# One inference step of a retention/convolution block with PEER expert retrieval on one core: the front reordered, a fence moved from slot 12 to slot 24, and every second key of the second table product computed as three float32r products

## The chip, the cores and the metric

The kernel runs on one core of one Trainium2 chip. A core has TensorE (PE in the profile, with its weight loads as PEld), VectorE (DVE), ScalarE (ACT), GpSimd (POOL) and SyncE (SP, here only a DMA queue), each with its own queue of instructions that it works through in order. The metric is the device time of one execution in microseconds (us). A profiled execution has a time of its own and a span, from its first to its last recorded instruction.

## The reference

Two batches go through one layer: a prompt of 512 tokens and 8 samples of 4 new tokens with kept states. D is 1024.

```python
def decoder_layer(x, r0, buf, ...):
    q, k, v, g, ca, cg = split(x @ w_in + b_in, 6)
    q, k = rope(q), rope(k) * DK ** -0.5
    o, r_new = retention(q, k, v, r0)              # 4 heads of 128, chunks of 128 tokens
    ret_out = silu(g) * head_norm(o)
    conv_out, buf_new = conformer_conv(ca, cg, buf)  # GLU, depthwise conv of 31 taps, layer norm, silu
    x = layer_norm(ALPHA * x + concat(ret_out, conv_out) @ w_out)
    return layer_norm(ALPHA * x + peer(x)), r_new, buf_new

def peer(x):                                       # 8 heads, 128 x 128 experts
    s1, s2 = q1 . sub_keys_1, q2 . sub_keys_2      # q = x @ w_query, two halves of 128 per head
    v1, i1, v2, i2 = top_k(s1, 16), top_k(s2, 16)
    sv, ci = top_k(v1 + v2 of all pairs, 16)
    idx = e1 * 128 + e2;  gate = softmax(sv)
    act = gelu(peer_u[idx] . x)
    return sum over 8 x 16 of gate * act * peer_v[idx]
```

So for each token 128 of 16,384 experts are chosen; the score with a row of peer_u is passed through gelu, multiplied by the gate, and weights a row of peer_v. All data are float32.

## The kernel before

The 544 tokens are handled in four parts: the first 128 prompt tokens (group 0), the 32 sample tokens (group s), 128 further prompt tokens (group b) and the last 256 prompt tokens (ND = 256, the dense part). The program is recorded in the order of the code, and a scheduler then puts the instructions of each engine into a fixed order by its own estimates. Each engine works in that order, so an instruction that waits holds up all that stand behind it on its engine. SP's and POOL's queues, which issue the DMAs, are held up in the same way.

**The front** (to about 490 us) computes retention, convolution and the first norm. Group 0 goes first, alone, so that its experts are known early. Then, for the other tokens: `glu` and `conv`, `project_v`, `rope` for q and k (it projects, rotates and writes qT and kT), `retain(c)` for chunks 1 to 3 (`scores`, `k_tokens`, `attend`, `advance`, `head_norm`), `silu_gate` (projects g), `conv_norm`, `gate_heads` (multiplies the normed heads into gT), and for each of four pieces of tokens `mix_a` (products with w_out) and `mix_b` (layer norm, transposition into x1T, L486 and L487). The powers in `head_norm` and `layer_norm` (L183 and L184) run on POOL, on the same queue as the gathers' DMAs.

**Groups 0, s and b: gathers.** `gather` walks through slots. For each slot POOL issues an indirect DMA (L572) that fetches, for 128 partitions, one row of 8 KB each (peer_u and peer_v side by side): 1.05 MB. DVE takes the dot product with x1 (L575, "dot"), ACT applies gelu and the gate (L579, L580), DVE adds the weighted second half into acc (L585). The buffers are three of the pool gp and, for every fourth slot, one of the pool gx (later gx2). Group 0 has 128 slots, group s 32 (four heads' quarters side by side on the partitions) and group b 128; s and b are the generator `fetched`. The fence: dots of group s from slot FREE on, and all dots of group b, are ordered on DVE behind the last instruction of `first_keys`.

**The dense part.** For the last 256 tokens all 16,384 experts are computed, 128 second-table keys of 128 experts each. For key e, `scores_of` loads 128 rows of peer_u (0.52 MB) into a buffer of the pool uvp (four buffers, UV) and multiplies with x1T (L784, 8 products of 128x256, "score row" here); gelu of it goes into the key's place in one of four stores: Ga (44 keys, 52 to 95), Gb (32, 0 to 31), Gc (20, 32 to 51) and Gd (32, 96 to 127). `build` makes the gates: for eight tokens a time ACT makes A (L862, L864), DVE makes M and B (L866, L870), PE multiplies (L875), and the result is multiplied into the stores (L899, L901) or copied (L911). `first_keys` does this for keys 0 to 95 and computes the score rows of Gc on the way; `last_keys` does it for 96 to 127. `s_stage` makes the score row of a key of Gd and multiplies it in (L883, L886). `v_stage` loads 128 rows of peer_v (0.52 MB, uvp too) and accumulates four products of 128x512 (L920) into the four banks pB; "table product" here.

`phases` runs the table products of keys 0 to 31, then closes gb, opens gd for Gd, and runs keys 32 to 95 with `last_keys` and, when it has ended, one `s_stage` per key beside them; then keys 96 to 127. `run` records one step of `phases` and two slots of `fetched` in turn. At the end two halves of 128 tokens are normed out of pB and stored.

Of the kernel before, what the change touches and what calls it, by code (L numbers as in the profile page):

```python
# [19 lines left out]
D = 1024  # L20
# [14 lines left out]
UV = 4  # L35
FREE = 12
# [57 lines left out]
def tile_step(ctx: ExitStack, tc: tile.TileContext, a, o):  # L94
# [736 lines left out]
    gbs = ExitStack()  # L831
    gb = gbs.enter_context(tc.tile_pool(name="gb", bufs=1, side="right", reuse_waits="tile"))
# [10 lines left out]
    gc = ctx.enter_context(tc.tile_pool(name="gc", bufs=1, reuse_waits="tile"))  # L843
# [70 lines left out]
    def v_stage(e):  # L914
        vt = uvp.tile([128, D], F32, name="uv")
        nc.sync.dma_start(vt, a["uv"][e * NK:(e + 1) * NK, D:])
        W = place(e)
        for b in range(2):
            for q in range(2):
                T.matmul(pB[b][q], W[:, b * 128:(b + 1) * 128], vt[:, q * 512:(q + 1) * 512],  # L920
                         start=False, stop=(e == NK - 1), skip_group_check=True)

    def phases():
        for e in range(EG[0]):
# [15 lines left out]
        for e in range(E0S[3], NK):  # L940
            v_stage(e)
            yield

# [74 lines left out]
```

## Time and profile before

| | us |
|---|---|
| median of 3 runs | 1602.21 |
| lowest, highest | 1598.4, 1611.17 |
| profiled execution: time | 1603.19 |
| profiled execution: span | 1601.4 |
| TensorE busy in the span | 1494.5 (93%) |
| VectorE busy | 1225.3 (77%) |
| ScalarE busy | 604.3 (38%) |
| GpSimd busy | 374.1 (23%) |
| moved by DMA | 503.75 MB, mean 315 GB/s |

The busy times are sums over the span; since the stages of this kernel have different limits, a table by stretches of the span says more. In the groups of instructions a row gives line, engine, operation, what is written and read, shapes and count, then the busy time in us and the mean length of one in ns, and then the idle time of the engine just before these instructions with what ended it. A matrix product in f32 stands as two records, and records of PE overlap, so that busy time over count is nearer to the pace than the mean length. The waits name who waited for whom, the sum in us, how often, and the longest. The chain of waits is followed back from the last instruction; a row gives start, length and what.

### The profile page before, as it was taken

To read this page: it belongs to the slowest core of one execution; us is meant where nothing else is said; L and a number is where in the kernel's file an instruction comes from. 1 tells how busy PE (TensorE), PEld (TensorE's weight loads), DVE (VectorE), ACT (ScalarE), POOL (GpSimd) and SP (SyncE) were. 2 spreads that over 40 slices of the span, in tenths; PEclk is the share of its full clock that TensorE was granted. 3 is DMA by queue.
4 is the path that set the end of the run, shared out by engine and by line. 5 is a ranking of instruction groups with operands and counts; after the bars stand their busy time and mean duration, and the time that the engine had idled before them with its cause. 6 is when DMAs were issued, how large, how long until landed. Compare 5 with 4: busy or idle time off the path is not lost.

```text
span 1601.4 us, 20802 instructions
## 1 busy us (share of the span) xinstructions
PE 1494.5 (93%) x7014; PEld 1010.1 (63%) x7014; DVE 1225.3 (77%) x3158; ACT 604.3 (38%) x1687; POOL 374.1 (23%) x335
## 2 busy tenths in 40 slices
PE   6899999996979999999999997999999999999996
PEld 6788556564756667788788875444566655543332
DVE  3939989989865999999852788566777777766666
ACT  2235542254222323333623888413994111111111
POOL 1001423444321222321120000122223222222221
PEclk9899999998989999999999997999999999999998
DMA  9458778997698669997794321998999999999995
GB/s 355 180 195 347 253 280 301 354 364 253 253 383 321 260 250 340 345 340 271 251 413 157 108 86 57 398 402 332 385 365 380 423 424 424 424 423 424 424 424 211
DMA packets 99543, 503.75 MB, mean 315 GB/s; under 512 B 10183, under 2 KB 21191, under 8 KB 56549
## 3 DMA queue, kind: packets, MB, share of 16 engines
q0 software_dynamic: 42240, 305.12, 48.7%
q1 hardware_dynamic: 50749, 189.96, 31.3%
q10 hardware_dynamic: 6448, 7.36, 1.5%
q8 instruction: 55, 0.90, 0.2%
q14 instruction: 51, 0.42, 0.1%
HBM read 497.03 MB, written 5.80 MB: 314 GB/s over the span
## 4 chain that ended last, share of the span: by engine, by line
PE 32%; DMA 28%; DVE 24%; issue 8%; ACT 4%; POOL 2%; SPq 0%; DVEq 0%; POOLq 0%; ACTq 0%
DMA g<-in_uv_dram,Ib 17%; PE pB L920 10%; PE sp L784 9%; PE mm L198 7%; DMA g<-in_uv_dram,I 7%; DVE acc L585 6%; DVE g L575 4%; POOL g L572 2%; ACT off L862 2%; PE mm L875 2%; PE mm L308 2%; DMA g<-in_w_in_dram 2%; DMA uv<-in_uv_dram 1%; DVE iu L504 1%; DVE score L505 1%
## 5 line engine op out<-in xcount | busy, mean ns | idle before, releaser
L784 PE MATMUL sp<-x1T,uv 128*128 128x256 f32 x2048 | 464.7, 384 | 15.4 <-ACT Ga L830 9.4
L784 PEld LDWEIGHTS sp<-x1T,uv 128*128 128x128 f32 x2048 | 385.5, 191 | 89.5 <-issue 23.2
L585 DVE SCALAR_TENSOR_TENSOR acc<-g,wgt,acc 128x1024 f32<-128x1024 f32 x285 | 365.0, 1281 | 99.3 <-ACT wgt L580 98.1
L572 POOL DMA_INDIRECT g<-in_uv_dram,I x128 | 181.9, 1421 | 435.1 <-DVE acc L585 222.6
L579 ACT ACTIVATE act<-act 128x1 f32<-128x1 f32 x288 | 57.9, 201 | 592.4 <-DVE g L575 592.0
L575 DVE SCALAR_TENSOR_TENSOR g<-g,x1g 128x1024 f32<-128x1024 f32 x160 | 195.3, 1224 | 94.2 <-DMA g<-in_uv_dram,Ib 63.1
L572 POOL DMA_INDIRECT g<-in_uv_dram,Ib x128 | 133.5, 1043 | 517.9 <-DVE acc L585 318.5
L575 DVE SCALAR_TENSOR_TENSOR g<-g,x 128x1024 f32<-128x1024 f32 x128 | 155.6, 1217 | 31.9 <-DMA g<-in_uv_dram,I 31.8
L198 PE MATMUL mm<-x1T,w 128*128 128x384 f32 (+1 forms) x512 | 176.1, 500 | 0.2 <-ACT score L524 0.2
L920 PE MATMUL pB<-uv,Ga 128*128 128x512 f32 x352 | 162.1, 604 | 1.1 <-DMA uv<-in_uv_dram 0.8
L862 ACT ACTIVATE off<-row,e1T 128x128 bf16<-128x128 bf16 x512 | 157.8, 388 | 1.5 <-PE mm L875 0.4
L198 PEld LDWEIGHTS mm<-x1T,w 128*128 128x128 f32 x512 | 96.6, 190 | 71.4 <-issue 37.9
L920 PE MATMUL pB<-uv,Gd 128*128 128x512 f32 x256 | 117.2, 601 | 2.1 <-DMA uv<-in_uv_dram 1.0
L920 PE MATMUL pB<-uv,Gb 128*128 128x512 f32 x256 | 115.4, 604 | 2.9 <-DMA uv<-in_uv_dram 2.5
L920 PEld LDWEIGHTS pB<-uv,Ga 128*128 128x128 f32 x352 | 63.7, 189 | 83.7 <-issue 63.1
L920 PEld LDWEIGHTS pB<-uv,Gd 128*128 128x128 f32 x256 | 46.1, 189 | 73.3 <-issue 48.2
L875 PEld LDWEIGHTS <-A 128*128 128x128 bf16 x1536 | 64.6, 100 | 36.6 <-issue 32.0
L920 PEld LDWEIGHTS pB<-uv,Gb 128*128 128x128 f32 x256 | 48.1, 193 | 59.6 <-issue 54.3
L875 PE MATMUL mm<-B,A 128*128 128x96 bf16 (+1 forms) x1536 | 68.4, 197 | 13.3 <-DVE Gc L901 12.4
L864 ACT ACTIVATE A<-off 128x1024 bf16<-128x1024 bf16 x64 | 67.4, 1053 | 28.1 <-PE mm L875 27.7
L870 DVE TENSOR_TENSOR B<-M,gtT 128x768 bf16<-128x768 bf16 (+1 forms) x192 | 69.8, 419 | 9.8 <-PE mm L875 9.6
L920 PE MATMUL pB<-uv,Gc 128*128 128x512 f32 x160 | 72.3, 599 | 0.0
(279 smaller groups left out, 1706.3 us busy)
## 6 DMA issues: line engine op xcount, KB each, us to landing
uv<-in_ut_dram SPq DMA_DIRECT2D x128, 512.0 KB
uv<-in_uv_dram SPq DMA_DIRECT2D x128, 512.0 KB
w<-in_w_in_dram SPq DMA_DIRECT2D x18, 1024.0 KB
w<-in_w_query_dram SPq DMA_DIRECT2D x16, 1024.0 KB
w<-in_w_out_dram SPq DMA_DIRECT2D x7, 1024.0 KB
g<-in_uv_dram,I POOLq DMA_INDIRECT x128, 7.9
keys<-in_state_retention_dram ACTq DMA_DIRECT2D x4, 512.0 KB
out_dram<-keys SPq DMA_DIRECT2D x4, 512.0 KB
```

What stands on the lines that cost most here:

```text
L198: T.matmul(p[:, :n], w[m // 2][:, k, (m % 2) * 128:(m % 2 + 1) * 128], xT[:, k, c0:c0 + n], start=(k == 0), stop=(k == 7))
L308: mm = T.matmul(p[:n, q * 256:(q + 1) * 256], xT[:, k, c0:c0 + n], w[q][:, k, :], start=(k == 0), stop=(k == 7))
L572: G.indirect_dma_start(out=t, out_offset=None, in_=a["uv"], in_offset=bass.IndirectOffsetOnAxis(ap=idx[:, k:k + 1], axis=0))
L575: dot = V.scalar_tensor_tensor(t[:, :D], t[:, :D], 1.0, x1, op0=OP.mult, op1=OP.mult, accum_out=act[:, 0:1])
L579: S.activation(act[:, 1:2], act[:, 0:1], AF.Gelu)
L585: V.scalar_tensor_tensor(acc, v, wgt, acc, op0=OP.mult, op1=OP.add)
L784: T.matmul(sp, u[:, k], x1T[:, k, NG2:], start=(k == 0), stop=(k == 7))
L862: S.activation(off[:, t], row, AF.Abs, bias=e1T[:, t1 + t:t1 + t + 1])
L864: S.activation(A, off, AF.Relu, bias=1.0, scale=-1.0)
L870: V.tensor_tensor(B[:, q], M, pairs_of(gtT[:, q], t1).to_broadcast([128, TB // 2, ne, 2]), op=OP.mult)
L875: T.matmul(pt[:, t % nt], A[:, t - t1], B[:, q, (t - t1) // 2, :, t % 2], start=(q == 0), stop=(q == 2))
L920: T.matmul(pB[b][q], W[:, b * 128:(b + 1) * 128], vt[:, q * 512:(q + 1) * 512], start=False, stop=(e == NK - 1), skip_group_check=True)
```

## The change

Front: `silu_gate` and the copy of the samples' gates are recorded ahead of `rope`; w_out is loaded earlier, `conv_norm` stands ahead of the three `retain`, which now follow each other; `mix_a` for the first two pieces stands ahead of the gates of chunks 2 and 3. The first block of w_query is projected in two steps, the columns up to the last 128 tokens first.

Fence: FREE goes from 12 to 24. The buffer gx2 moves to the other side of the memory. Gd takes over the store of Gb and gd is gone.

Table products: from key 52 on, when Gc has been used up and its room is given to a new pool, every even key up to 122 is split. ACT copies the loaded rows and the key's weights into float32r tiles (vh, Wh), DVE subtracts these from the originals into two more (vl, Wl), and twelve products of 128x512 in float32r (low weights by high rows, high by low, high by high) take the place of four in f32. The parts are made two keys ahead, from a pool of three buffers. The last four keys are loaded together, and are recorded with the first half of the tokens ahead of the second. The final norm writes into a buffer of gp.

```diff
-FREE = 12
+FREE = 24
...
+    silu_gate(load_win(3), xT, n - NS, [(0, n - NS, gT[:, :, r])], False)
+    S.activation(gT[:, :, s_], gS, AF.Copy)
     rope(load_win(0), 0, xT, n - NS, 160, [(0, n - NS, qT)])
-    rope(load_win(1), 1, xT, n - NS, 160, [(0, n - NS, kT)])
-    wg = load_win(3)
+    wk_ = load_win(1)
+    wo = load_w(a["w_out"], 0)
+    rope(wk_, 1, xT, n - NS, 160, [(0, n - NS, kT)])
+    wo += load_w(a["w_out"], 512)
+    S.activation(y[:, :, s_], yS, AF.Copy)
+    conv_norm(y, n)
...
     retain(1)
     retain(2)
-    banks[:] = [ps]
-    silu_gate(wg, xT, n - NS, [(0, n - NS, gT[:, :, r])], False)
-    wo = load_w(a["w_out"], 0) + load_w(a["w_out"], 512)
-    S.activation(y[:, :, s_], yS, AF.Copy)
-    conv_norm(y, n)
-    S.activation(gT[:, :, s_], gS, AF.Copy)
+    retain(3)
...
     gate_heads(ons[1], C, gT, NS)
-    gate_heads(ons[2], C, gT, NS + C)
-    retain(3)
-    gate_heads(ons[3], C, gT, NS + 2 * C)
     mix_a(0, NS, None)
     mix_a(NS, C, 0)
+    gate_heads(ons[2], C, gT, NS + C)
+    gate_heads(ons[3], C, gT, NS + 2 * C)
...
-        for m in range(4):
-            S.activation(qs[:, h0 * 2 + m], project(w, m, x1T, 0, n), AF.Copy)
+        for c0, c1 in ((0, n - C), (n - C, n)) if h0 == 0 else ((0, n),):
+            for m in range(4):
+                S.activation(qs[:, h0 * 2 + m, c0:c1], project(w, m, x1T, c0, c1 - c0), AF.Copy)
...
-    def v_stage(e):
+    def v_row(e):
         vt = uvp.tile([128, D], F32, name="uv")
         nc.sync.dma_start(vt, a["uv"][e * NK:(e + 1) * NK, D:])
-        W = place(e)
+        return vt
+
+    vhp, split, rows = [], lambda e: e % 2 == 0, {}
+
+    def v_ready(e):
+        vt, W = v_row(e), place(e)
+        if not vhp or not split(e):
+            rows[e] = ((W, vt),)
+            return
+        vh, vl = vhp[0].tile([128, D], F32R, name="vh"), vhp[0].tile([128, D], F32R, name="vl")
+        S.activation(vh, vt, AF.Copy)
+        V.tensor_sub(vl, vt, vh.bitcast(F32))
+        Wh, Wl = vhp[0].tile([128, ND], F32R, name="Wh"), vhp[0].tile([128, ND], F32R, name="Wl")
+        S.activation(Wh, W, AF.Copy)
+        V.tensor_sub(Wl, W, Wh.bitcast(F32))
+        rows[e] = ((Wl, vh), (Wh, vl), (Wh, vh))
+
+    def v_products(e, b):
+        terms = rows[e]
+        for w, v in terms:
+            for q in range(2):
+                T.matmul(pB[b][q], w[:, b * 128:(b + 1) * 128], v[:, q * 512:(q + 1) * 512], start=False, ...)
+
+    def v_stage(e):
+        if e not in rows:
+            v_ready(e)
         for b in range(2):
-            for q in range(2):
-                T.matmul(pB[b][q], W[:, b * 128:(b + 1) * 128], vt[:, q * 512:(q + 1) * 512], ...)
+            v_products(e, b)
...
-        gbs.close()
-        gd = ctx.enter_context(tc.tile_pool(name="gd", bufs=1, side="right", reuse_waits="tile"))
-        GW[3] = gd.tile([128, EG[3], ND], F32, name="Gd")
+        GW[3] = GW[0]
...
         for e in range(E0S[1], E0S[3]):
+            if e == 52:
+                gcs.close()
+                vhp.append(ctx.enter_context(tc.tile_pool(name="vhp", bufs=3, reuse_waits="tile")))
+            if vhp and split(e + 2):
+                v_ready(e + 2)
             v_stage(e)
...
-        for e in range(E0S[3], NK):
+        for e in range(E0S[3], NK - UV):
+            if split(e + 2) and e + 2 < NK - UV:
+                v_ready(e + 2)
             v_stage(e)
             yield
+        split = lambda e: False
+        for e in range(NK - UV, NK):
+            v_ready(e)
+        for b in range(2):
+            for e in range(NK - UV, NK):
+                v_products(e, b)
+                yield
...
-    gx2.append(ctx.enter_context(tc.tile_pool(name="gx2", bufs=1, reuse_waits="tile")))
+    gx2.append(ctx.enter_context(tc.tile_pool(name="gx2", bufs=1, side="right", reuse_waits="tile")))
...
-        t = uvp.tile([128, D], F32, name="uv")
+        t = gp.tile([128, 2 * D], F32, name="g")[:, :D]
```

More of the change, by code (lines that the diff above doesn't have):

```diff
@@ L842, in tile_step @@
     dw_ = ctx.enter_context(tc.tile_pool(name="dw_", bufs=4, reuse_waits="tile"))
-    gc = ctx.enter_context(tc.tile_pool(name="gc", bufs=1, reuse_waits="tile"))
+    gcs = ExitStack()
+    gc = gcs.enter_context(tc.tile_pool(name="gc", bufs=1, reuse_waits="tile"))
     pacc = ctx.enter_context(tc.tile_pool(name="pacc", bufs=1, space=PSUM, reuse_waits="tile"))
@@ L912, in last_keys @@
                 yield
-    def v_stage(e):
+    def v_row(e):
         vt = uvp.tile([128, D], F32, name="uv")
         nc.sync.dma_start(vt, a["uv"][e * NK:(e + 1) * NK, D:])
-        W = place(e)
+        return vt
[16 more added lines that the diff above has]
+            for q in range(2):
+                T.matmul(pB[b][q], w[:, b * 128:(b + 1) * 128], v[:, q * 512:(q + 1) * 512], start=False,
+                         stop=(e == NK - 1 and w is terms[-1][0] and v is terms[-1][1]), skip_group_check=True)
+    def v_stage(e):
+        if e not in rows:
+            v_ready(e)
         for b in range(2):
-            for q in range(2):
-                T.matmul(pB[b][q], W[:, b * 128:(b + 1) * 128], vt[:, q * 512:(q + 1) * 512],
-                         start=False, stop=(e == NK - 1), skip_group_check=True)
+            v_products(e, b)
     def phases():
+        nonlocal split
         for e in range(EG[0]):
```

3 lines of the change are left out of this document (1 added, 2 removed).

## The prediction

> **What bounds the kernel now.** I read the busy shares first, then a table of stages, then the chain of waits in the last stages, then the groups of instructions that the change touches. The whole span says only that TensorE (PE) has little idle time; the stages say more. The page's two lines come first (busy us and share; GB/s in 40 slices of 40 us); then the table: stretch and length; busy us of PE, weight loads, VectorE (DVE), ScalarE (ACT), GpSimd (POOL); granted clock; DMA share; GB/s.
>
> ```profile
> PE 1494.5 (93%) x7014; PEld 1010.1 (63%) x7014; DVE 1225.3 (77%) x3158; ACT 604.3 (38%) x1687; POOL 374.1 (23%) x335
> ...
> GB/s 355 180 195 347 253 280 301 354 364 253 253 383 321 260 250 340 345 340 271 251 413 157 108 86 57 398 402 332 385 365 380 423 424 424 424 423 424 424 424 211
> ```
>
> ```profile
> 350.00:492.00 142.00, 112.21 (x508) 81.93 (x507) 109.39 (x184) 45.65 (x118) 51.40 (x45) 0.90 0.83 309
> 492.00:780.00 288.00, 275.95 (x1223) 217.61 (x1221) 269.18 (x1071) 98.15 (x242) 64.14 (x52) 0.99 0.80 291
> ...
> 875.00:912.00 37.00, 36.58 (x324) 32.47 (x322) 25.58 (x98) 27.57 (x77) 0.00 (x0) 1.00 0.39 126
> 912.00:992.00 80.00, 64.72 (x633) 54.05 (x629) 67.79 (x254) 71.28 (x199) 0.00 (x0) 0.87 0.17 55
> 992.00:1205.00 213.00, 211.88 (x1172) 108.25 (x1173) 148.42 (x278) 129.59 (x379) 55.83 (x49) 0.99 0.94 369
> 1205.00:1409.00 204.00, 201.43 (x738) 124.53 (x737) 149.53 (x202) 45.31 (x158) 56.71 (x55) 1.00 1.01 416
> 1409.00:1586.00 177.00, 174.00 (x381) 68.20 (x379) 120.44 (x146) 23.35 (x94) 40.32 (x44) 1.00 0.97 404
> ```
>
> From 992 to 1205 PE is full and DMA has room (369 GB/s). From 1205 on both are full; which one gives the pace shows in the chain of waits (start, us, what):
>
> ```profile
> 1240.27 10.96 DMA g<-in_uv_dram,Ib
> 1253.08 1.30 DVE acc L585
> 1254.64 11.43 DMA g<-in_uv_dram,Ib
> ...
> 1565.83 1.30 DVE acc L585
> 1567.38 12.36 DMA g<-in_uv_dram,Ib
> ```
>
> The chain is gathers: land, dot, accumulate, reissue. The chain shows one round of the four gather buffers per pair of lines: 21 rounds from 1254.64 to 1567.38, 14.9 us each, 3.72 us a gather. Up to 1409 a round moves four gathers of 1.05 MB (128 rows of 8 KB), two table rows and two score rows of 0.52 MB: 6.29 MB, 422 GB/s, and the page's slices stand at 424. **DMA is the pace from 1205 on; PE only keeps up.** With 424 GB/s as the ceiling a gather is 2.47 us, a row 1.24.
>
> **The change, part by part.**
>
> *Float32r products.* The rows for a price (columns: busy, mean ns | idle before):
>
> ```profile
> L920 PE MATMUL pB<-uv,Ga 128*128 128x512 f32 x352 | 162.1, 604 | 1.1 <-DMA uv<-in_uv_dram 0.8
> L784 PE MATMUL sp<-x1T,uv 128*128 128x256 f32 x512 | 117.6, 383 | 2.4
> L875 PE MATMUL mm<-B,A 128*128 128x96 bf16 x768 | 44.3, 218 | 13.3 <-DVE Gc L901 12.4 <-DVE Gc L899 0.9
> L875 PE MATMUL mm<-B,A 128*128 128x32 bf16 x768 | 24.1, 176 | 0.0
> L920 PEld LDWEIGHTS pB<-uv,Ga 128*128 128x128 f32 x352 | 63.7, 189 | 83.7 <-issue 63.1
> 1035.97 44.73 PE pB L920 x104
> ```
>
> An f32 product is two records. Back to back they run at 44.73 / 104 = 0.43 us, so a key (8 records) is 3.44 us and each record takes 0.84 ns a column; a score row (16 records of 117.6 / 512 = 0.23) is 3.68. The bf16 rows differ by (57.7 - 31.4) ns over 64 columns: 0.41 ns a column. So an f32 product streams as four bf16-like passes. No row shows float32r. Bounds per product: 0.19 us (the weight load, which must hide behind it), 0.22 (one bf16-like pass), 0.43 (one f32 record), 0.86 (no gain). I take 0.22: three products that leave out only low by low replace four passes. A split key is then 12 x 0.22 = 2.64 us, 0.80 less; 36 keys (52, 54 ... 122) save 29 us of PE. The Trainium skill (FP8 and Floating Point Precision, TensorE Precision Notes) says that true fp32 makes four passes of high and low parts and that a reduced reading truncates 4 bytes to 22 bits; by that the product is one pass, and the four in the trace agree. [...]
>
> *Making the parts.* Per split key two subtractions and two copies, by
>
> ```profile
> 1588.18 1.22 DVE L454 TENSOR_TENSOR yt<-yt,lng 128x1024 f32<-128x1024 f32 x1
> L886 DVE TENSOR_TENSOR Gd<-Gd,W 128x256 f32<-128x256 f32 x32 | 13.1, 422 | 1.8 <-ACT W L883 1.7
> 1586.90 1.24 ACT L453 ACTIVATE yt<-yt,lrs 128x1024 f32<-128x1024 f32 x1 [5.34 <-DVE lrs L451]
> L883 ACT ACTIVATE W<-sp 128x256 f32<-128x256 f32 x32 | 12.2, 380 | 52.0 <-PE sp L784 51.2 <-DVE Gd L886 0.8
> ```
>
> 1.64 us of DVE and 1.62 us of ACT a key. DVE is idle 54 of 204 and 57 of 177 us, ACT far more: the 59 us fit, at no cost to the sum. What counts is the order: DVE issues in order, so a key's subtraction sits between gathers' dots, and PE cannot run ahead of the gathers by more than the two keys of lead.
>
> *Fence at 24.* Twelve more gathers of group s go into the stretch after 835, where the queue now stands still:
>
> ```profile
> POOL g L572 <- DVE Gc L899: 157.0, 1, 157.0
> DVE Gb L899 <- ACT Gb L835: 24.4, 1, 24.4
> L585 DVE SCALAR_TENSOR_TENSOR acc<-g,wgt,acc 128x1024 f32<-128x1024 f32 x102 | 131.1, 1285 | 51.8 <-ACT wgt L580 51.7
> L575 DVE SCALAR_TENSOR_TENSOR g<-g,x1g 128x1024 f32<-128x1024 f32 x101 | 123.7, 1225 | 56.5 <-DMA g<-in_uv_dram,Ib 56.3
> ```
>
> In the changed program's built order seven of the twelve dots stand ahead of the first multiplication by the built weights, five among the first steps of it. Seven at 3.7 us fill 26 us, against the 24.4 us that DVE waits there now: +2. The five cost 2.6 us of DVE each in a stretch where PE's score rows set the pace (875 to 912: 11 us of DVE idle in 37): +2. Bounds 0 and 12 x 2.6 = 31; I take **+4**. After the fence 12 gathers fewer are left.
>
> *Front.* PE idles 30 us between 350 and 492:
>
> ```profile
> PE mm L339 <- ACT on L332: 14.2, 2, 12.6
> PE mm L486 <- DVE xr L455: 11.2, 1, 11.2
> L198 PE MATMUL mm<-x1T,w 128*128 128x416 f32 x256 | 91.1, 513 | 0.2 <-ACT score L524 0.2
> L198 PE MATMUL mm<-g,w 128*128 128x128 f32 x256 | 30.2, 275 | 0.0
> 469.62 22.61 PE L198 MATMUL mm<-x1T,w 128*128 128x416 f32 x64
> ```
>
> The second wait is the last norm; the new split of the first w_query block (288 columns, then 128) puts 64 x 0.356 x 288/416 = 15.8 us of products over it and leaves 64 x 0.118 = 7.6 behind it, 0.6 more in all. The first wait is head_norm's, whose power runs on POOL. silu_gate's products, which partly covered retain, are now ahead of it, and retain(3) stands before the gates: part of the wait can come back elsewhere. On POOL the last norm's power moves from behind the 42nd to behind the 44th gather after the sample head's; 42 took
>
> ```profile
> 291.03 1.05 POOL L184 TENSOR_TENSOR hrs<-hrs,mhalf 32x4 f32<-32x4 f32 x1
> ...
> 458.46 0.57 POOL L184 TENSOR_TENSOR lrs<-lrs,mhalf 128x1 f32<-128x1 f32 x1
> ```
>
> 167 us, 4.0 each, so the last columns come some 8 us later, at about 477 instead of 469, and PE ends the block at 485 instead of 492 (last row: 469.6 + 22.6). I take **-8** (bounds -27, both waits gone, and +8, none). It carries on, since 492 to 912 is PE at 96 to 100%.
>
> *Stages from the fence.* Dots of the 160 slots of groups s and b, counted in DVE's built order: before 12 to the fence, then 48 to the last build step, 54 to the last score row, 46 to the end; after 24, 48, 58, 30. Keys at the two inner points are about 54 and 82 in both.
>
> - To the last build step: same work, PE-bound, 213 us. Ends 1205 - 8 + 4 = 1201.
> - To the last score row: (58 x 1.049 + 54 x 0.524) = 89.1 MB at the row's 416 GB/s = **214** us (before 54 x 1.049 + 54 x 0.524 = 84.9 MB in 204). PE needs only 14 x (2.64 + 3.44 + 7.36) = 188, so the 14 split keys here gain nothing. Ends 1415.
> - To the last dot: 30 gathers and 31 rows, 47.7 MB, 112.5 us by DMA at 424, 95 by PE (15.5 pairs of 6.1). Ends at 1527.5; before, 1579.8 (row below).
> - Then five split keys (114 to 122), whose subtractions stand behind the last dot, and nine plain ones: 6 us until the first parts are there (dot, accumulation and two subtractions: 1.23 + 1.28 + 0.42 + 1.22, and the waits between), then 5 x 2.64 + 9 x 3.44 = 44. Before, only 7 us of PE lay behind that dot.
> - End: one layer norm and the store, 15 us now; the last key still does both halves in the built order, so 13.5.
>
> ```profile
> 1579.76 1.23 DVE L575 SCALAR_TENSOR_TENSOR g<-g,x1g 128x1024 f32<-128x1024 f32 x1 [0.54 <-DMA g<-in_uv_dram,Ib]
> 1568.33 18.19 PE L920 MATMUL pB<-uv,Gd 128*128 128x512 f32 x40 [1.01 <-DMA uv<-in_uv_dram]
> 1594.66 1.29 DVE L455 TENSOR_TENSOR uv<-uv,lnb 128x512 f32<-128x512 f32 x2
> ```
>
> On SP the store of group b now stands ahead of the last seven rows' loads. It waits for the norm, some 15 us behind the last dot; PE needs row 121 only 27 us behind it: covered, 0. The move of gx2, the reuse of Gb and the tiles' return to gp change no instruction's length: 0.
>
> Sum: 1527.5 + 6 + 44 + 13.5 = 1591 of span, against 1601.4; the profiled execution's time is 1.8 above its span and 1.0 above the median of the three runs, so **1592**. The gathers end 52 us earlier, and 42 of it is lost again: the keys left behind them have DMA idle and PE alone.
>
> **The rivals.**
>
> 1. *Better balance, 1566.* If the front loses both waits (-27 instead of -8) and parts come early enough for PE to run three keys ahead (the pool has three buffers: 7 us), 1592 - 19 - 7 = 1566. For it: DMA at 0.72 to 0.83 in the front; against it: POOL's order, and DVE's.
> 2. *Slower: float32r is bound by the 4-byte stream.* At 0.43 a product a split key is 5.2 us, 2.5 more than taken. To the last score row PE needs 14 x (5.2 + 3.44 + 7.36) = 224, +10; to the last dot 15.5 x 8.64 = 134, +21; behind it 5 x 2.5 = +13: 1636. It decides once a product costs over about 0.32 us, where a split and a plain key together pass DMA's 7.26 us a pair (112.5 / 15.5). For it: the f32 records' 0.84 ns a column; against: four passes in two records. At 0.86 it would be some 1800; I hold that for 1 in 30.
> 3. *The fence's dots hold up the build.* All 31 us fall on the build, where ACT is busy 71 of 80 us: 1592 + 27 = 1619.
> 4. *It doesn't do what it says:* the twelve gathers stay behind the fence on POOL's queue. Then the last dot comes 12 x 3.7 = 44 us later and PE has finished more beside it: about 1600.
>
> **How the numbers follow.** Forecast 0.55, between 1568 and 1605 (half of the front's bounds either way, and 5 us on each of the two DMA stages); rival 1 0.20; rival 2 0.14; rival 3 0.07; rival 4 0.04. A measurement of this kernel can tell about 1% from no change, 16 us: faster is below 1586, slower above 1618. The forecast lies 6 us inside; two fifths of its chance (0.22) are faster, the rest (0.33) within 1%. Faster 0.22 + 0.20 = 0.42; within 0.33 + half of rival 3 + rival 4 = 0.40; slower 0.14 + half of rival 3 = 0.18. Range 1563 to 1634: to rival 1 and nearly all of rival 2.
>
> **What would show it.** In the changed profile: L941's float32r records near 0.22 us; gathers at 3.7 us and DMA at 416 to 424 GB/s between the last build step and the last dot, with PE idle there for the first time; the last dot near 1528, and behind it some 60 us in which DMA falls to rows alone; the fence some 4 us behind its shifted place. Wrong it would be by a float32r record of 0.4 us, by a front that ends before 475 or after 495, or by keys that are not tied to the dots, so that both end together.

## The result, and the profile after

The changed kernel takes 1615.41 us (median of 5 runs, 1610.14 to 1618.93) against 1602.21: 13 us more by the medians; the ratio over the runs is **1.0067 [1.0040, 1.0094]**, which makes some 11 us. 1592 was forecast. The profiled execution took 1618.93 us with a span of 1617.1, 3.5 above the median; before, it was 1.0 above.

First the page of the changed kernel: busy times, and GB/s in 40 slices of 40 us.

```profile
PE 1471.1 (91%) x7222; PEld 1052.2 (65%) x7222; DVE 1272.6 (79%) x3230; ACT 651.5 (40%) x1763; POOL 415.2 (26%) x335
...
GB/s 362 168 198 346 242 284 293 371 337 239 263 362 319 262 248 342 339 331 246 254 396 379 233 79 68 377 358 422 341 361 372 411 423 422 422 420 415 402 263 90
```

PE is busy 23 us less than before, and yet the kernel is slower. The last slices answer the shape that was forecast: DMA is full up to the last dot, then falls to 263 and 90, where before it stood at 424 up to the last slice (211). Now the table by stages, cut at this kernel's own points: end of the first w_query block, last multiplication by the built weights (the fence), last build step, last score row, last dot, last product. Columns as in the table of before: busy us of PE, weight loads, DVE, ACT, POOL; granted clock; DMA share; GB/s.

```profile
350.00:514.50 164.50, 123.85 (x639) 98.17 (x638) 122.94 (x206) 48.70 (x135) 61.53 (x49) 0.88 0.78 292
514.50:912.00 397.50, 385.41 (x1863) 313.75 (x1862) 347.73 (x1229) 153.04 (x411) 81.32 (x74) 0.99 0.84 313
912.00:1003.60 91.60, 80.35 (x797) 67.95 (x796) 80.11 (x303) 83.75 (x231) 0.45 (x1) 0.90 0.22 73
1003.60:1216.30 212.70, 208.28 (x1169) 103.25 (x1169) 150.15 (x279) 133.36 (x388) 57.58 (x50) 0.99 0.95 366
1216.30:1435.40 219.10, 198.73 (x804) 144.37 (x803) 177.50 (x240) 63.26 (x189) 79.45 (x59) 0.98 1.01 412
1435.40:1552.40 117.00, 101.92 (x304) 58.13 (x305) 95.48 (x121) 34.47 (x91) 42.26 (x27) 0.96 1.00 404
1552.40:1605.40 53.00, 53.00 (x158) 29.41 (x156) 17.11 (x25) 7.74 (x11) 1.41 (x4) 1.00 0.41 138
```

| stage | forecast, us | measured, us | difference |
|---|---|---|---|
| fence ends at | 988 | 1003.6 | +15.6 |
| to the last build step | 213 | 212.7 | -0.3 |
| to the last score row | 214 | 219.1 | +5.1 |
| to the last dot | 112.5 | 117.0 | +4.5 |
| PE alone | 50 | 53.0 | +3.0 |
| norm and store | 13.5 | 11.7 | -1.8 |
| span | 1591 | 1617.1 | +26.1 |

Three fifths of the miss had happened by the fence; the rest lies where float32r and the gathers run side by side. The front's own rows on PE (start, length, and in brackets the idle time before it and what ended it):

```profile
460.69 0.66 PE L486 MATMUL mm<-cst,keys 128*128 128x128 f32 x4 [2.07 <-DVE keys L455]
...
482.50 1.09 PE L486 MATMUL mm<-cst,xr 128*128 128x128 f32 x4 [19.32 <-DVE xr L455]
...
486.82 15.80 PE L198 MATMUL mm<-x1T,w 128*128 128x288 f32 x64 [0.68 <-ACT on L428]
502.46 4.91 PE L784 MATMUL sp<-x1T,uv 128*128 128x256 f32 x22
507.21 7.31 PE L198 MATMUL mm<-x1T,w 128*128 128x128 f32 x64
```

The wait for the last norm is 19.3 us, before 11.2: the 288 columns meant to lie over it stand behind the norm's transposes (L486) in PE's fixed order. The block ends at 514.5; before 492.2, forecast 485. Not all of these 22 us are lost: score rows of 4.9 us now stand between the two steps, and up to the block's end PE idles 71 us, before 57, so that 14 of the 22 are idle time and the rest is work that comes earlier. What held the norm up stands in DVE's order:

```profile
464.16 1.23 DVE L575 SCALAR_TENSOR_TENSOR g<-g,x 128x1024 f32<-128x1024 f32 x1 [1.72 <-DMA g<-in_uv_dram,I]
...
469.13 1.23 DVE L575 SCALAR_TENSOR_TENSOR g<-g,x 128x1024 f32<-128x1024 f32 x1 [3.74 <-DMA g<-in_uv_dram,I]
...
471.48 0.69 DVE L447 BATCH_NORM_STATS2 lst<-mm 128x6 f32<-128x512 f32 x1
...
474.11 1.23 DVE L575 SCALAR_TENSOR_TENSOR g<-g,x 128x1024 f32<-128x1024 f32 x1 [0.75 <-DMA g<-in_uv_dram,I]
...
475.26 0.69 DVE L447 BATCH_NORM_STATS2 lst<-mm 128x6 f32<-128x512 f32 x1
```

PE's products for that norm were done at 458.6 (444.65 + 13.98). The first statistics come at 471.5, because two dots stand ahead of them that wait for gathers to land, and the second behind a third dot.

### The profile page after: what moved, and what is told of

It reads as the page before. It is cut to its first block, busy times and chain, and to the rows that moved or that the text cites. A ratio compares the mean times of both kernels' runs of the same rounds, so it can differ in the third digit from the quotient of the medians.

```text
span 1617.1 us, 21373 instructions
## 1 busy us (share of the span) xinstructions
PE 1471.1 (91%) x7222; PEld 1052.2 (65%) x7222; DVE 1272.6 (79%) x3230; ACT 651.5 (40%) x1763; POOL 415.2 (26%) x335
## 4 chain that ended last, share of the span: by engine, by line
PE 31%; DVE 26%; DMA 23%; issue 9%; ACT 7%; POOL 4%; SPq 0%; DVEq 0%; POOLq 0%; ACTq 0%
PE sp L784 12%; PE pB L941 8%; DMA g<-in_uv_dram,I 6%; DVE acc L585 6%; PE mm L198 6%; DVE g L575 5%; DMA uv<-in_uv_dram 5%; DMA g<-in_uv_dram,Ib 4%; DMA uv<-in_ut_dram 3%; POOL g L572 3%; ACT off L863 3%; DMA g<-in_uv_dram,Is 2%; PE mm L876 2%; DMA g<-in_w_in_dram 2%; ACT A L865 1%
## 5 line engine op out<-in xcount | busy, mean ns | idle before, releaser
L784 PE MATMUL sp<-x1T,uv 128*128 128x256 f32 x2048 | 466.1, 384 | 29.0 <-DMA uv<-in_ut_dram 15.5
L572 POOL DMA_INDIRECT g<-in_uv_dram,I x128 | 173.9, 1358 | 436.4 <-DVE acc L585 238.7
L572 POOL DMA_INDIRECT g<-in_uv_dram,Ib x128 | 174.2, 1361 | 426.5 <-DVE acc L585 276.6
L575 DVE SCALAR_TENSOR_TENSOR g<-g,x1g 128x1024 f32<-128x1024 f32 x160 | 195.5, 1224 | 47.2 <-DMA g<-in_uv_dram,Is 28.4
L941 PE MATMUL pB<-uv,Gb 128*128 128x512 f32 x400 | 184.4, 610 | 7.0 <-DMA uv<-in_uv_dram 6.3
L198 PE MATMUL mm<-x1T,w 128*128 128x384 f32 (+3 forms) x576 | 176.5, 464 | 0.7 <-ACT on L428 0.7
L198 PEld LDWEIGHTS mm<-x1T,w 128*128 128x128 f32 x576 | 104.7, 191 | 67.0 <-issue 29.9
L941 PEld LDWEIGHTS pB<-uv,Gb 128*128 128x128 f32 x400 | 75.2, 194 | 99.0 <-issue 79.9
L941 PE MATMUL pB<-uv,Ga 128*128 128x512 f32 x176 | 82.6, 613 | 9.0 <-DMA uv<-in_uv_dram 9.0
L941 PE MATMUL pB<-uv,Gc 128*128 128x512 f32 x160 | 74.5, 612 | 0.0
L198 PE MATMUL mm<-g,w 128*128 128x160 f32 (+1 forms) x512 | 70.4, 296 | 1.3 <-DMA w<-in_w_in_dram 1.3
L198 PEld LDWEIGHTS mm<-g,w 128*128 128x128 f32 x512 | 68.0, 198 | 2.4 <-DMA w<-in_w_in_dram 1.6
L572 POOL DMA_INDIRECT g<-in_uv_dram,Is x32 | 34.0, 1063 | 130.0 <-DVE acc L585 84.6
```

Of the source, the lines that this page charges most:

```text
L198: T.matmul(p[:, :n], w[m // 2][:, k, (m % 2) * 128:(m % 2 + 1) * 128], xT[:, k, c0:c0 + n], start=(k == 0), stop=(k == 7))
L572: G.indirect_dma_start(out=t, out_offset=None, in_=a["uv"], in_offset=bass.IndirectOffsetOnAxis(ap=idx[:, k:k + 1], axis=0))
L575: dot = V.scalar_tensor_tensor(t[:, :D], t[:, :D], 1.0, x1, op0=OP.mult, op1=OP.mult, accum_out=act[:, 0:1])
L784: T.matmul(sp, u[:, k], x1T[:, k, NG2:], start=(k == 0), stop=(k == 7))
L941: T.matmul(pB[b][q], w[:, b * 128:(b + 1) * 128], v[:, q * 512:(q + 1) * 512], start=False, stop=(e == NK - 1 and w is terms[-1][0] and v ...
```

## The experiments

Each ratio is to the kernel before, run beside it on the same chip. One profile is one execution, and executions of one kernel differ by 4 to 9 us either way (free24_only: 1590 to 1608, and its profile is the 1590); also, an edit anywhere can change the built order elsewhere. Even the fence, with the same code ahead of it, is passed at 994 to 1005 in the profiles with the new front and the fence at 24, and at 982 to 994 with the old front. So the verdicts go by the ratios, and the profiles show mechanisms.

| kernel | us | ratio and interval |
|---|---|---|
| changed kernel | 1615.41 | 1.0067 [1.0040, 1.0094] |
| old_front | 1605.69 | 1.0014 [0.9999, 1.0028] |
| no_split | 1609.17 | 1.0030 [1.0010, 1.0051] |
| front_only | 1608.92 | 1.0033 [1.0018, 1.0047] |
| free24_only | 1599.42 | 0.9973 [0.9956, 0.9990] |
| norm_first | 1608.68 | 1.0038 [1.0018, 1.0058] |
| no_two_step | 1624.74 | 1.0147 [1.0113, 1.0180] |
| late_split | 1597.31 | 0.9968 [0.9949, 0.9987] |
| parts_only | 1662.53 | 1.0363 [1.0325, 1.0400] |
| rows_ahead | 1615.92 | 1.0053 [1.0026, 1.0080] |
| high_only | 1598.79 | 0.9968 [0.9945, 0.9992] |
| late_norm | 1599.98 | 0.9971 [0.9949, 0.9994] |
| fourth_key | 1615.01 | 1.0056 [1.0037, 1.0075] |
| every_key | 1603.19 | 1.0001 [0.9982, 1.0019] |
| free32_late | 1608.94 | 1.0013 [0.9997, 1.0029] |
| every_old | 1596.34 | 0.9965 [0.9944, 0.9986] |
| every_old_norm | 1598.38 | 0.9960 [0.9937, 0.9982] |

### The three parts of the change, one at a time

Without the new front:

```diff
-    silu_gate(load_win(3), xT, n - NS, [(0, n - NS, gT[:, :, r])], False)
     rope(load_win(0), 0, xT, n - NS, 160, [(0, n - NS, qT)])
...
     retain(2)
-    retain(3)
+    banks[:] = [ps]
+    silu_gate(wg, xT, n - NS, [(0, n - NS, gT[:, :, r])], False)
...
-        for c0, c1 in ((0, n - C), (n - C, n)) if h0 == 0 else ((0, n),):
```

> The changed kernel with the front of before (the order of the retention, gates and mixing, and one 416-column pass for the first w_query block); the fence at 24 and the float32r keys stay. Theory 1, the front costs the change its gain: the first w_query block ends at 492 again instead of 514.5, the fence's first dots stand near 993 to 997 instead of 1003, and the time is 1598 to 1606 instead of 1615. Theory 2, the front's loss is taken up by slack before the fence and the loss sits behind it: the time stays at 1612 to 1618.

Without float32r:

```diff
-    vhp, split, rows = [], lambda e: e % 2 == 0, {}
+    vhp, split, rows = [], lambda e: False, {}
```

> The changed kernel with every key as plain float32 products, so no high and low parts are made; all else stays. Theory 1, the gathers' DMA sets the pace up to the last dot and float32r pays only in the keys behind it: 5 keys by 0.7 us, 1617 to 1621. Theory 2, PE is the bound and the 36 keys' saving counts whole: 36 x 0.7 = 25 us, 1640. Theory 3, the parts cost more than the products save, since DVE's subtractions stand between the dots: 1600 to 1610.

The kernel before with the new front alone (the same lines the other way round):

> The kernel before with nothing but the reordered front and the w_query block in two steps; fence at 12, no float32r. Theory 1, the front alone is slower: the first w_query block ends near 514 instead of 492, the fence some 10 us later, the time 1610 to 1622 against 1602. Theory 2, the front is neutral to the end: 1598 to 1606.

The kernel before with the fence alone:

```diff
-FREE = 12
+FREE = 24
```

> The kernel before with nothing but the fence at slot 24. Theory 1, the gathers end some 40 us earlier and the keys left behind them have PE alone: last dot near 1536 to 1542, 13 to 15 plain keys (3.44 us each) behind it, 1592 to 1602. Theory 2, the twelve gathers' dots hold up the build whole (12 x 2.6 = 31 us before the fence): the fence near 1023 and the time 1610 to 1620.

Theory 1 holds for the front in old_front (1605.7; the block ends at 499.9, later than the 492 expected, the fence at 994.0). For front_only its range is a little too high (1608.9; block end 509.6), and the fence, at 993.8, is 1 us later than before and not 10. By the ratios the front costs 0.53% in one and 0.33% in the other, **5 to 9 us**, not the 22 us by which its block is late. For float32r theory 3 holds: without it the kernel is 0.37% faster, so **float32r on every second key costs some 6 us**; with intervals of 0.27% and 0.20% either way this is barely clear of nothing. The fence alone gains 0.27%, and its first theory holds (last dot at 1519.7, earlier still than expected, but in a profile 9 us faster than the median). The sums agree within the intervals: -4 for the fence, +5 to +9 for the front and +6 for float32r make +7 to +11, and +11 was measured.

Why the fence gains only 4 us although it ends the gathers up to 60 us earlier (1579.8 before), three rows of free24_only show:

```profile
1195.50:1403.40 207.90, 205.72 (x727) 125.45 (x725) 151.59 (x205) 43.31 (x152) 57.21 (x56) 1.00 1.01 416
1403.40:1519.70 116.30, 115.47 (x252) 45.19 (x253) 78.70 (x96) 15.81 (x63) 27.48 (x29) 1.00 1.01 421
1519.70:1576.90 57.20, 57.20 (x134) 25.04 (x132) 10.03 (x15) 1.74 (x3) 1.37 (x4) 1.00 0.41 139
```

PE is busy 321 of 324 us beside the gathers and 57 of 57 behind them. With plain products both engines are full and PE's sum sets the end: from the fence to the last product it is 594.7 us, before 594.0. The gain shows behind that product, 11.7 us to the end against 14.9.

### The front

The dots of the first gathers from slot 72 on are ordered behind the last norm:

```diff
+            if x1 is x1_0 and k >= 72:
+                behind(dot, lnl[-1])
```

> The changed kernel, with the dots of the first gathers from slot 72 on ordered behind the last norm of the front on DVE (an order alone, no work added). Theory 1, the front's loss is DVE's order: the last norm's statistics stand behind dots that wait for gathers. Then PE's wait for that norm falls from 19.3 us to 7 to 10, the first w_query block ends near 503 instead of 514.5, and the time is 1605 to 1611 instead of 1615. Theory 2, it is GpSimd's order (the norm's power behind gathers that wait for buffers): the wait stays above 15 us and the time at 1612 to 1618.

norm_first, PE's wait for that norm:

```profile
464.86 1.08 PE L488 MATMUL mm<-cst,xr 128*128 128x128 f32 x4 [4.92 <-DVE xr L457]
```

Theory 1: the wait is 4.9 us and the block ends at 493.8, 21 us earlier. DVE's order made it, not POOL's. The ratio falls by 0.29%, 5 us, but the two intervals overlap, so that this gain isn't clear of nothing.

The w_query block in one pass, in the new front:

```diff
-        for c0, c1 in ((0, n - C), (n - C, n)) if h0 == 0 else ((0, n),):
-            for m in range(4):
-                S.activation(qs[:, h0 * 2 + m, c0:c1], project(w, m, x1T, c0, c1 - c0), AF.Copy)
+        for m in range(4):
+            S.activation(qs[:, h0 * 2 + m], project(w, m, x1T, 0, n), AF.Copy)
```

> The changed kernel with the first w_query block in one pass of 416 columns again; the rest of the new front stays. Theory 1, the split hides nothing, because in PE's order the 288 columns stand behind the last norm's transposes: PE's wait for that norm stays at 18 to 21 us and the time is 1612 to 1618. Theory 2, the split hides its 16 us and the loss is elsewhere in the front: without it the time is 1622 to 1632.

no_two_step on PE:

```profile
481.52 1.09 PE L486 MATMUL mm<-cst,xr 128*128 128x128 f32 x4 [19.02 <-DVE xr L455]
...
485.84 24.65 PE L198 MATMUL mm<-x1T,w 128*128 128x416 f32 x64 [0.68 <-ACT on L428]
```

The wait is as long as with the split, and the block ends at 510.5 against 514.5: the split hides nothing, as theory 1 has it. The time, 1624.7, lies in theory 2's range all the same, 0.8% above the changed kernel, but not by its mechanism: the fence is passed at 1002.5, 1 us earlier than there, so the loss lies behind it (last dot at 1557.0 against 1552.4), where only the built order can differ. It isn't explained.

The same order with the old front (and with float32r for the late keys, next section):

```diff
+            if x1 is x1_0 and k >= 70:
+                behind(dot, lnl[-1])
```

> Fence at 24, the front of before, float32r for the keys 112 to 123 alone, and the dots from slot 70 on ordered behind the front's last norm. If DVE's order at that norm costs the old front too (11 to 15 us of PE's wait there), the time falls from 1597 to 1588 to 1594; if the old front hides it, 1595 to 1600.

late_norm, then late_split, which differs from it in this order alone:

```profile
463.76 0.94 PE L488 MATMUL mm<-cst,xr 128*128 128x128 f32 x4 [4.29 <-DVE xr L457]
```

```profile
468.87 1.09 PE L486 MATMUL mm<-cst,xr 128*128 128x128 f32 x4 [14.67 <-DVE xr L455]
```

Ten microseconds less of PE's wait, and nothing at the end (0.9971 against 0.9968). So some of what PE loses in the front is slack. A likely reason, which no run tests: from 492 to 780 DVE is busy 269 of 288 us before the change, PE 276, so that the choice of the experts on DVE may pace part of that stretch.

### What float32r costs

Float32r only for the keys 112 to 123, all of them, with the old front:

```diff
-    vhp, split, rows = [], lambda e: e % 2 == 0, {}
+    vhp, split, rows = [], lambda e: e >= 112, {}
```

> Fence at 24 with the front of before, and float32r only for the keys 112 to 123, every one of them: ten of the twelve have their parts behind the last dot, where PE works alone. Theory 1, float32r pays exactly where PE is alone and costs where the gathers run: against about 1600 for this kernel without any float32r, ten keys by 0.7 us less, 1591 to 1596. Theory 2, the parts cost as much as the products save there too: 1598 to 1603.

1597.3, 0.46% below old_front, where the even keys from 52 on are split, and 1 us above theory 1's range. It is hardly better than the fence alone (0.9968 against 0.9973): where PE works alone float32r does no harm, and its gain of ten times 0.7 us can't be told from nothing here.

Making the parts, and multiplying with the plain rows:

```diff
-        for w, v in terms:
+        for w, v in terms[:1] and plain(e):     (plain(e) is the key's weights and its row as loaded)
```

> The changed kernel makes the high and low parts of the 36 keys, but multiplies with the plain float32 rows and weights, so the parts are never read. Theory 1, making the parts (DVE and ACT between the gathers' dots) is what slows the stretch with the gathers: it is as slow as in the changed kernel, and the keys behind the last dot are plain ones again, 1615 to 1621. Theory 2, the products' tie to the parts is what slows it: the gathers go as without float32r, 1607 to 1612.

Neither. The gathers end as early as without float32r (last dot at 1539.9, in no_split at 1543.4), but PE is busy only 278 us of the 325 up to there and has 114 us left behind the last dot, twice as much as the changed kernel:

```profile
1216.30:1541.10 324.80, 278.46 (x901) 166.12 (x900) 266.55 (x363) 92.65 (x285) 124.10 (x86) 0.95 0.99 402
1541.10:1655.00 113.90, 109.53 (x250) 48.09 (x249) 25.07 (x29) 15.98 (x17) 0.80 (x3) 0.97 0.40 136
```

Making parts costs PE some 46 us of waiting in that stretch, even when it doesn't need them; 28 us of it the score rows wait for ACT (W, L884). (In this form a row's buffer is held for the subtraction and the product both, longer than in the changed kernel, so its size isn't the changed kernel's.)

The rows of the plain keys asked for earlier:

```diff
-            if vhp and split(e + 2):
-                v_ready(e + 2)
+            if vhp:
+                for k in range(e + 1, e + 3):
+                    if k not in rows:
+                        v_ready(k)
...
```

> The changed kernel with the plain keys' rows also asked for up to two keys ahead, in the order of the keys, so that SP no longer asks for a split key's row before the plain key's that is needed earlier; products, parts and bytes stay. Theory 1, the order of the rows starves PE: the stretch from the last build step to the last dot, 336 us in the changed kernel and 327 without float32r, falls to 326 to 330, and the time to 1604 to 1609. Theory 2, the gathers' DMA or DVE's order sets that stretch: it stays at 333 to 338 and the time at 1612 to 1618.

Theory 2: 1615.9. PE now waits for the parts (vh, 21 us between 1218 and 1545) in place of the table rows (15 us in the changed kernel).

The subtractions and the low parts left out, so that a split key is one float32r product of the high parts. This form serves to read the time; it lacks two of the three products:

```diff
-        V.tensor_sub(vl, vt, vh.bitcast(F32))
-        V.tensor_sub(Wl, W, Wh.bitcast(F32))
-        rows[e] = ((Wl, vh), (Wh, vl), (Wh, vh))
+        rows[e] = ((Wh, vh),)
```

> [...] ACT's two copies, the rows and their order stay; DVE loses 36 x 1.65 us and PE two of three products. Theory 1, DVE's subtractions between the dots slow the gathers: from the last build step to the last dot 325 to 329 us instead of 336, and five keys behind it by 1.8 us less, 1595 to 1600. Theory 2, it is the copies, the rows or DMA: the stretch stays at 333 to 338 and only the keys behind the last dot gain, 1604 to 1609.

The stretch is 338 us, as theory 2 has it, and the keys behind the last dot take 36 us instead of 53; the time, 1598.8, is lower than theory 2 said. The groups between 1218 and 1545 show what DVE and ACT waited for (busy, mean ns | idle before, what ended it). no_split, the changed kernel, high_only, every_key:

```profile
L585 DVE SCALAR_TENSOR_TENSOR acc<-g,wgt,acc 128x1024 f32<-128x1024 f32 x88 | 113.1, 1285 | 47.5 <-ACT wgt L580 47.5
L575 DVE SCALAR_TENSOR_TENSOR g<-g,x1g 128x1024 f32<-128x1024 f32 x88 | 107.7, 1224 | 43.3 <-DMA g<-in_uv_dram,Ib 43.1
```

```profile
L585 DVE SCALAR_TENSOR_TENSOR acc<-g,wgt,acc 128x1024 f32<-128x1024 f32 x87 | 111.7, 1284 | 41.5 <-ACT wgt L580 41.5
L575 DVE SCALAR_TENSOR_TENSOR g<-g,x1g 128x1024 f32<-128x1024 f32 x86 | 105.5, 1227 | 3.9 <-DMA g<-in_uv_dram,Ib 3.8
L931 DVE TENSOR_TENSOR vl<-uv,vh 128x1024 fp32r<-128x1024 f32 x30 | 36.9, 1229 | 6.6 <-ACT vh L930 6.6
```

```profile
L585 DVE SCALAR_TENSOR_TENSOR acc<-g,wgt,acc 128x1024 f32<-128x1024 f32 x86 | 110.5, 1285 | 74.5 <-ACT wgt L580 74.5
L575 DVE SCALAR_TENSOR_TENSOR g<-g,x1g 128x1024 f32<-128x1024 f32 x85 | 104.0, 1223 | 19.0 <-DMA g<-in_uv_dram,Ib 18.7
L930 ACT ACTIVATE vh<-uv 128x1024 fp32r<-128x1024 f32 x30 | 31.6, 1054 | 48.3 <-DMA uv<-in_uv_dram 48.3
```

```profile
L585 DVE SCALAR_TENSOR_TENSOR acc<-g,wgt,acc 128x1024 f32<-128x1024 f32 x82 | 105.2, 1283 | 21.8 <-ACT wgt L580 21.8
L575 DVE SCALAR_TENSOR_TENSOR g<-g,x1g 128x1024 f32<-128x1024 f32 x81 | 99.3, 1225 | 0.9 <-DMA g<-in_uv_dram,Ib 0.9
L931 DVE TENSOR_TENSOR vl<-uv,vh 128x1024 fp32r<-128x1024 f32 x64 | 78.1, 1220 | 2.6 <-ACT vh L930 2.6
```

Without float32r DVE has two idle times: 47.5 us until ACT's weight is there, half a microsecond in every gather, and 43 us until gathers land. With 30 keys' parts (37 us and 13 for the weights) the second is gone, 3.9 us, and the first has hardly shrunk, 41.5: **DVE has next to no room left beside the gathers.** In every_key, where the parts are twice as many, the first is filled too, down to 21.8 us, while the gathers get slower. That DVE alone paces them isn't shown: in parts_only it makes the same parts, and the gathers end as early as without, beside 15 table rows fewer in DMA. In high_only DVE has less to do, but ACT's copies wait 48 us for rows, and the wait for the gathers' weights, which ACT makes too, grows from 41.5 to 74.5.

Half of the split keys, and twice as many:

```diff
-    vhp, split, rows = [], lambda e: e % 2 == 0, {}
+    vhp, split, rows = [], lambda e: e % 4 == 0, {}     (fourth_key)
+    vhp, split, rows = [], lambda e: True, {}           (every_key)
```

> The changed kernel with every fourth key split instead of every second. Theory 1, DVE's time sets the stretch from the last build step to the last dot: without float32r DVE waits 43 us there for gathers to land, and the parts of every second key (30 keys by 1.65 us) use that up and more; half as many (25 us) fit. Then DVE waits 15 to 20 us for gathers again, the stretch takes 325 to 330 us instead of 336, and the time is 1606 to 1612. Theory 2, it is not DVE's time: the stretch stays at 333 to 338 and the time at 1614 to 1618.

> The changed kernel with every key from 52 to 123 split. Theory 1, DVE's time: a gather costs DVE 3.13 us (dot, accumulation and the wait for the weight), 88 of them 275, the score rows' multiplications 13, the parts of some 57 keys 94: the stretch takes 370 to 395 us, few keys are left behind the last dot, and the time is 1620 to 1640. Theory 2, DMA sets the stretch: 334 to 340 us, and the keys behind the last dot all gain, 1608 to 1613.

fourth_key, between 1218 and 1545:

```profile
L575 DVE SCALAR_TENSOR_TENSOR g<-g,x1g 128x1024 f32<-128x1024 f32 x86 | 105.5, 1227 | 17.2 <-DMA g<-in_uv_dram,Ib 16.8
```

In fourth_key DVE waits 16.8 us for gathers, as theory 1 has it, and the stretch is 332 us by DVE's last build step (324 by ACT's copy of its result); but the time, 1615.0, is no better. So DVE's room alone doesn't set the time. For every_key both theories fail. The gathers do get slower (353 us; DVE's wait for them 0.9), which fits DVE's time; but the keys don't stay behind: only 24 us follow the last dot, against 53, and the time is 1603.2. In the same 327 us the loads that were issued, changed kernel and then every_key:

```profile
uv<-in_uv_dram SPq DMA_DIRECT2D x60, 512.0 KB
uv<-in_ut_dram SPq DMA_DIRECT2D x27, 512.0 KB
g<-in_uv_dram,Ib POOLq DMA_INDIRECT x85
```

```profile
uv<-in_uv_dram SPq DMA_DIRECT2D x65, 512.0 KB
uv<-in_ut_dram SPq DMA_DIRECT2D x27, 512.0 KB
g<-in_uv_dram,Ib POOLq DMA_INDIRECT x81
```

Four gathers less and five rows more: DMA is shared out otherwise, and the PE-only end shrinks. My expectation had taken the longer stretch as a loss, without the keys done in it.

What both theories left out is PE's own sum. From the fence to the last table product, in the profiled executions:

| kernel | keys split | us | PE busy | PE idle |
|---|---|---|---|---|
| no_split | none | 597.5 | 586.5 | 11.0 |
| fourth_key | 18 | 607.6 | 571.5 | 36.1 |
| changed kernel | 36 | 601.8 | 561.9 | 39.9 |
| every_key | 72 | 592.0 | 544.8 | 47.2 |

The waiting comes with the first split keys and grows little with their number, while what the products save grows with it: 15, 25 and 42 us less to do, against 25, 29 and 36 us more idle. So a quarter and half of the keys lose (the ratios can't tell these two apart), and all of them gain.

### Towards a faster version

```diff
-FREE = 24
+FREE = 32
-    vhp, split, rows = [], lambda e: e >= 112, {}     (of late_split)
+    vhp, split, rows = [], lambda e: e >= 104, {}
```

> Fence at 32 (all gathers of group s ahead of it), the front of before, float32r for the keys 104 to 123 alone, whose parts nearly all stand behind the last dot. If PE alone sets the time from the fence on, eight more keys at 0.7 us less than the version with the fence at 24: 1589 to 1595; if the eight gathers' dots hold up the build by their 2.6 us each, 1600 or more.

1608.9, the second case: the fence is passed at 1013.3, 23 us later than in late_split. So the prediction's third rival exists, but from somewhere between 24 and 32 on.

The old front of old_front with every_key's line, and then the order at the norm as in late_norm:

> Fence at 24, the front of before, and every key from 52 to 123 split. If the front's loss (1615 against 1606 with every second key) and the gain of splitting every key (1615 against 1603) are independent, 1591 to 1597, the fastest of the study; if every key split only makes up for the late start of the new front, 1600 to 1606.

> The same with the dots from slot 70 on ordered behind the front's last norm. If that wait counts to the end with the old front, 1586 to 1592; if, as with the fence at 24 and late keys, it comes to nothing, the same as without, 1591 to 1597.

1596.3 and 1598.4: the gains of the old front and of splitting every key add within the intervals, and the order at the norm again comes to nothing with the old front. every_old, late_split and free24_only all beat both kernels, by 0.27 to 0.35%, and can't be told from each other; the last is a change of one number.

## Why the prediction was wrong

- **The front** (taken at -8, bounds -27 and +8) is the step that failed first: at the end it costs 5 to 9 us. The block ended 22 us later than before, outside both bounds; the transposes of the last columns came 16.4 us later (482.5 against 466.1), not 8. The sum had put 15.8 us of products over the last norm's wait without looking where they stand in PE's order: behind the transposes. And it had taken the norm to be held by POOL's queue of gathers; it was DVE's, where three dots stand ahead of the statistics (norm_first). A second step failed the other way: "it carries on, since 492 to 912 is PE at 96 to 100%". Of 15 to 22 us at the block 5 to 9 are left at the end, part of them having been work moved ahead; the row quoted for it had DVE at 93%.
- **The parts at no cost** is the second. The 54 and 57 us of DVE's idle time were read as room; about half is the wait for ACT's weight within each gather. The price was known (1.23 + 0.42 us a key, as taken), the room was not: 43 us of waiting for gathers for 50 us of parts. The two stages took 9.6 us more than forecast, 336.1 in all; in no_split they take 327.2, close to the 326.5 of the forecast. So the parts cost 9 us there, and the split keys behind the last dot give 4 back (53.0 against 56.9), which fits the 6 us by the ratios. That PE would wait beside the gathers had been forecast (43 us by its sums; 35 measured).
- **The fence** (+4 for the build, bounds 0 and 31): no such delay shows beside the spread of single executions (with the old front it is passed at 982 in free24_only and at 994 in old_front, before at 992.5). Alone the move gains 4 us at the end.
- **DMA is the pace from 1205 on; PE only keeps up** was half right: beside plain products PE is as full as DMA (free24_only). That is why earlier gathers alone win so little.
- **The float32r product at 0.22** held. Two products start 0.45 us after the two before (1442.02 and 1442.47, below), 0.23 each; a split key takes 2.7 to 2.8 us. So rival 2 falls. If all 4 bytes of an element are read, 512 columns of 128 lanes in 0.23 us are 1140 GB/s. The Trainium skill (SBUF — State Buffer, SBUF: two separate sides) gives TensorE's port about 614 GB/s, for bf16 at 2 bytes a lane; for float32r that is no bound here.
- **The end as PE alone** held: 53 us against 50, DMA at 138 GB/s. Rival 1's idea, parts early enough for keys to run beside the gathers, isn't what happened with every second key; with every key it was nearer.
- The measured time lies between the bounds of the range only because these reach to rival 2, which didn't happen; that is luck.

What stays open is why PE's waiting grows at once by 25 to 36 us, with a quarter of the keys split by more than these save. In the mixed forms PE waits for table rows (22 us in fourth_key), in every_key for parts (37 us) and not for rows; asking for the rows earlier only changed one wait for the other. A trace of SP's queue points to the four row buffers: between 1218 and 1545 its loads wait for a buffer, and in no_split it is PE that ends all these waits (290 us), while in the changed kernel 97 of 292 us end with DVE's subtractions, which stand among the dots and of which one reads the row's buffer. No kernel with more row buffers was tried, so this isn't shown.

## What to carry to other kernels

Idle time of an in-order engine isn't all room of one kind: here 39 of the 43 us of waiting for gathers were filled first, while the wait inside each gather (0.5 us for the weight) was filled only with twice as many parts, and the gathers took 353 us instead of 327. So take such waits out before saying that work fits, and count what the other engines wait for the new work. What a faster product saves grows with the number of products changed; the waiting that it brings needn't. Products meant to cover a wait must be looked up in the engine's built order, since code that is recorded earlier can still be placed behind the wait. Between two full engines, giving one more room wins only what the other has left.

## What was not expected of the hardware

A short wait of PE costs more than itself. Changed kernel, PE, beside the gathers:

```profile
1442.02 0.62 PE L941 MATMUL pB<-vl,Wh 128*128 128x512 f32 x2
1442.47 0.61 PE L941 MATMUL pB<-vh,Wh 128*128 128x512 f32 x2
...
1479.41 3.70 PE L941 MATMUL pB<-uv,Ga 128*128 128x512 f32 x8 [0.98 <-DMA uv<-in_uv_dram]
...
1489.34 5.40 PE L941 MATMUL pB<-uv,Ga 128*128 128x512 f32 x8 [3.46 <-DMA uv<-in_uv_dram]
...
1535.59 6.67 PE L941 MATMUL pB<-uv,Gb 128*128 128x512 f32 x8 [2.98 <-DMA uv<-in_uv_dram]
```

A plain key is 3.70 us after a wait of 1 us, but 5.40 and 6.67 after waits of 3.5 and 3.0; the granted clock stood at 0.50 from 1490.4 to 1493.8 and from 1534.7 to 1541.6, and at 1.00 around these. The Trainium skill (TensorE: Matmul & The Clock Gate, Part 1: The HAM clock gate) says that the array falls to half its clock after an idle window of about 3.4 us and needs as long a busy one to rise. The rise agrees: the clock was halved for 3.4 and 6.9 us, about one and two such windows. The fall doesn't quite: one came 1.1 us after the wait of 3.46 us had ended, the other 2.1 us into the wait of 2.98 us, and in the 3.4 us ahead of them PE was busy for 1.1 and 1.2 us. So the window need not be wholly idle, and the measurement decides.

POOL's part of a gather also grew (spans on POOL are rough). no_split, the changed kernel, and high_only, which has no subtractions:

```profile
L572 POOL DMA_INDIRECT g<-in_uv_dram,Ib x85 | 88.3, 1039 | 227.5 <-DVE acc L585 224.8 <-DMA g<-in_uv_dram,Ib 2.7
```

```profile
L572 POOL DMA_INDIRECT g<-in_uv_dram,Ib x85 | 120.9, 1422 | 202.6 <-DVE acc L585 186.9 <-DMA g<-in_uv_dram,Ib 15.7
```

```profile
L572 POOL DMA_INDIRECT g<-in_uv_dram,Ib x84 | 121.4, 1445 | 201.4 <-DVE acc L585 191.6 <-DMA g<-in_uv_dram,Ib 9.8
```

1.04 us became 1.42 for one gather's issue. The Trainium skill (SBUF — State Buffer, SBUF: two separate sides) says that a DVE instruction with two inputs in SBUF and a GpSimd instruction that reads SBUF lock each other out of a port that they share. DVE's subtractions have two such inputs, but they aren't what lengthens the issue: without them it takes 1.45 us. What does stays open, and POOL still waits 187 us for buffers in the changed kernel.
